# Pauses per quarter and layer in a Hyena and attention encoder layer, later transposes of k, and another order of casts where two Strassen runs begin

## The chip, the core and the metric

The kernel runs on one core of one Trainium2 chip, in one launch. The metric is the time of that launch on the device, in microseconds (us). The engines are TensorE (PE: matrix products and transposes), VectorE (DVE), ScalarE (ACT), GpSimd (POOL) and SyncE (SP, which issues the loads of weights). Each engine has its own queue and works through it in order; one waits for another through semaphores.

## What is computed

One layer of an encoder on 512 tokens of 2048 channels, in float32. The normalised input goes through one projection to a Hyena branch (three blocks of 1024 channels), to attention (8 heads of q, 2 of k and v, 128 wide) and to two blocks of gates.

```python
h = rms_norm(x, mix_norm_g)
u_h, q, k, v, g = split(h @ w_in)
x0, x1, hv = split(centred_short_conv(u_h, hy_conv_w, hy_conv_b))
filt = implicit_filter(S, ...)            # a 3-layer sine MLP, then w4 and a decay
z = hv * x1
z = bidir_fft_conv(z, filt) + hy_bias * z
y_h = z * x0
y_a = attention(axial_rope(rms_norm(q)), axial_rope(rms_norm(k)), v)
g_h, g_a = split(sigmoid(g + b_gate))
x = x + (g_h * (y_h @ w_br_hyena) + g_a * (y_a @ w_br_attn)) @ w_out
h2 = rms_norm(x, ffn_norm_g)
return x + (silu(h2 @ w_ffn_gate) * (h2 @ w_ffn_up)) @ w_ffn_down
```

## The kernel before

Every float32 operand is split into a high part (a cast on ScalarE) and a low part (the difference, on VectorE), and a product is three matmuls: high by high, high by low, low by high (`mm3`). Weights come from one packed tensor, in blocks of 128 x 1024, on SyncE's queue; a block's raw tile is `wr`, its parts are `wh` and `wl`. The matmuls stand on TensorE in the order in which the code issues them. The other engines' orders are made by a scheduler from the program's order, from priorities and from `behind(ins)`, which keeps an instruction behind another one.

The stages are, in order of time: the projection's first tiles `px` with the norm's sum beside them; the rest of the Hyena projection, `px`, tile by tile, and the last `phv`; the chunk `kv`; q's chunk for group 0, a pair of gates, q's chunk for group 1; the branches' products `b`; the rest of the gates, as a Strassen-Winograd scheme of seven products (`seven`, tiles `gx`, `gy`, `gz`); the output projection `o`; the FFN's gate and up projections in the same scheme (`fx`, `fy`, `fz`); and the FFN's down projection `d`, `e`.

Beside these main groups runs side work: generators in a queue, of which `step()` (L143) advances one after each `mm3` of a main group. `yield n` in a generator makes it wait until n steps have passed; a step is one triple of matmuls. Up to the kv chunk the side work is: `mlp_gen` (L307), the MLP of three layers that makes the filter, where `hp` is a layer's product, `ha` its argument and `h` its sine, with a pause `MLP_WAIT` ahead of each layer and behind the last; `taps_gen`, the products `fp` of the MLP's output with w4, and the decay (`fd`, `bd`); a pause; and then, for each of four quarters of the channels, `filter_gen` (transposes `ktp`, tiles `kt`, their splits `k..h` and `k..l`, then the spectra `kp`), and the convolution (`ztp`, `up`, the products `cu` and `cv` with the spectrum, their transposed splits `Yt`, then `ab`). The next quarter's taps lie inside the one before. The norm's factor is broadcast by four small matmuls `rs1bcp`, which ScalarE copies to `rbc`.

Behind the kv chunk the side queue is flushed, and the code issues in this order: VectorE's squares of the norm's factor; the split of v (`vh` on ScalarE, `vl` on VectorE, L770 to L776); `rope_tables` for k (L646: two loads on ScalarE's queue, `rpk` with 512 KB and `gaink` with 128 KB, then eight products on GpSimd); and `norm_rope` for k (L657: squares `kscr`, the root `krt`, `kqn`, and the rotation to `ko`, half of it on GpSimd). `rpk` takes memory that the convolution's pool leaves, so whichever of `vh` and `rpk` is first on ScalarE waits for the last of the quarters. `k_gen` (L700) is side work inside the q chunk: K_WAIT steps, then the transposes `kT0p` and `kT1p` of ko. `attend_gen` (L706) transposes q's heads and makes the scores `sp`, whose softmax is `p` on ScalarE; it is side work too.

In `run` (L950), the first group of a Strassen run is issued while its operands are still being made. `V` holds the seven sums of the activations of one pair of channel blocks, `X` their parts; the last pair is number 7. `x_high` and `x_low` split parts a to b of a pair; `wsum` adds two weight tiles (`gs`, `fs`), `wsplit` splits a tile (`gwhs`, `gwls`, `fwhs`, `fwls`), and `fold` copies one half of a bank on ScalarE and adds the other on VectorE (`gv`, `fv`). The run of the gates splits the last pair in two pieces, 0 to 3 and 3 to 7, at once; the run of the FFN gets its last pair only when `o` is done (`sums()`), and inside it the second norm is summed (`norm`, `token_rstd`: `rs2ss`, `rs2a`, a root on ScalarE with a table load, `rs2dg`).

Of the kernel before, what the change touches and what calls it, by code (L numbers as in the profile page):

```python
# [23 lines left out]
NQ = 4  # L24
# [8 lines left out]
HYENA_LAST = 0, 13, 14, 15  # L33
ATT_LAST = 4, 5, 6, 7, 0, 1, 2, 3
G_EARLY = 7
MLP_WAIT = 18
Z_WAIT0 = 16
N_WARM = 10
XW = 4
RS_STEP = 8  # L40
K_WAIT = 20
Q_WAIT = (27, 28)
S_WAIT0 = 6
S_WAIT = 2
# [70 lines left out]
def layer_kernel(tc, wpk, xT, par, flt, zemb, w4, decT, tb2, rope, qkg, out):  # L115
# [46 lines left out]
    def queue(gen):  # L162
        side["queue"].append(gen)

    def pause(n):
        yield n
# [140 lines left out]
    def mlp_gen():  # L307


        hcur = zem  # L310
        yield MLP_WAIT
        w4_load(0)
        for l in range(3):
            nk = 33 if l == 0 else 64
            nr = 64 if l < 2 else P
            hp = ps_tile(f"hp{l}")
            mm(hp[:nr], fl[:nk, l * 64:l * 64 + nr], hcur[:nk], True, True)
            a = tmp(f"ha{l}")[:nr]
            nn = tmp(f"hn{l}")[:nr]
            nc.vector.tensor_scalar(a, hp[:nr], fl[:nr, 256 + l:257 + l], fl[:nr, 259:260], ALU.add, ALU.mult)  # L320
            nc.vector.tensor_scalar(nn, a, float(np.float32(1 / (2 * math.pi))), MAGIC, ALU.mult, ALU.add)
            nc.vector.tensor_scalar(nn, nn, MAGIC, None, ALU.subtract)
            for c in (C1, C2, C3):
                nc.vector.scalar_tensor_tensor(a, nn, -c, a, ALU.mult, ALU.add)
            nc.vector.tensor_scalar(a, a, PI32, -PI32, ALU.min, ALU.max)
            hcur = tmp(f"h{l}")[:nr]
            nc.scalar.activation(hcur, a, AF.Sin)
            if l == 2:

                hh, hl = cw("hh", [P, S], "hh", dt=F32R), cw("hl", [P, S], "hl", dt=F32R)  # L330
                nc.scalar.copy(hh, hcur)
                nc.vector.tensor_tensor(hl, hcur, hh.bitcast(F32), ALU.subtract)
                mlp["h"] = hh, hl
            yield MLP_WAIT
            if l == 0:
                w4_parts(0)

# [57 lines left out]
    def filter_gen(q):  # L395
# [17 lines left out]
            yield 3  # L413
        if q + 1 < NQ:
            w4_parts(q + 1)
        yield 9

        kd[q] = dpool.tile([256, 6 * 256], F32, tag=f"kd{q}", bufs=1, name=f"kd{q}")
        spectra = [], []
# [31 lines left out]
    def conv_gen(q):  # L451
# [37 lines left out]
                yield 5  # L489
        if q + 1 < NQ:  # L490
            yield from taps_gen(q + 1)
        yield 11 if q + 1 < NQ else 14
        abs_ = [work(f"abs{2 * q + c}") for c in range(2)]
        for ph in range(2):
            ab = [ps_tile(f"ab{q}{ph}{c}") for c in range(2)]
# [32 lines left out]
    xg, acc1 = [], work("acc1")  # L528
    queue(mlp_gen())
    queue(taps_gen(0))  # L530
    queue(pause(18))
    queue(filter_gen(0))
    w00 = wblk()
    for k in range(KT):
# [171 lines left out]
    def attend_gen(g, qr):  # L706
# [3 lines left out]
        qT = []  # L710
        for h in range(4):
            qT.append(head_T(qr, h, "qTh", "qTl", 4, f"qT{g}{h}"))
            yield 2
        pr, pt = {}, {}

        def scores(u):
# [102 lines left out]
    def seven(nm, gi, nv=3, turns=False, early=NEARLY):  # L819
# [73 lines left out]
        def wsplit(w, name, ins=None, low_ins=None):  # L893
            hi = wpool.tile([P, BLK * P], F32R, tag="whi", bufs=3, name=f"{nm}wh{name}")
            lo = wpool.tile([P, BLK * P], F32R, tag="wlo", bufs=3, name=f"{nm}wl{name}")
            with behind(ins):
                nc.scalar.copy(hi, w)  # L897
            with behind(low_ins):
                raws["wl"] = nc.vector.tensor_tensor(lo, w, hi.bitcast(F32), ALU.subtract).ins  # L899
            return hi, lo  # L900
# [49 lines left out]
        def run(groups, c_tiles, finish, rows=None, sums=None, side_pool=None, norm=None, tail=None, each=None, halves=False,  # L950
# [17 lines left out]
            for n in range(groups):  # L968
# [8 lines left out]
                if first:  # L977
# [5 lines left out]
                    ready = NP - 1 if sums else NP  # L983
                    s1 = wsum(f"s1_{n}", w0["a21"], w0["a22"])
                    for p in range(early, ready):
                        x_split(p, V[p], (0, 7) if p < NP - 1 else (0, 3, 7))
                        if p == (early if sums else NP - 1):
                            s2 = wsum(f"s2_{n}", s1, w0["a11"], raws["xl"])
                    rest(raws["xl"] if sums else raws["sum"])
# [14 lines left out]
                elif not sums:  # L1004
                    s4 = wsum(f"s4_{n}", s2, w0["a12"], v1a)
                hs1 = wsplit(s1, f"s1_{n}", raws["x"] if first else None)
                if ready < NP:
                    product(y, hs1, 2, True, 0, ready, part="high")
                else:
                    product(y, hs1, 2, True, 0, ready, swap=turn(n))  # L1010
                if ready < NP:
                    V[ready] = sums()
                    v6 = raws["v6"]
                    x_split(ready, V[ready], (0, 3))
                    s4 = wsum(f"s4_{n}", s2, w0["a12"], v6)
                    x3 = raws["x"]
                    x_high(ready, V[ready], 3, 7)
                    product(x, h11, 0, True, ready)
                    product(y, hs1, 2, True, 0, ready, part="low")
                    product(y, hs1, 2, True, ready)  # L1020
                    v1 = fold(f"v1_{n}", x)
                    x_low(ready, V[ready], 3, 4, raws["folda"])
                    hs2 = wsplit(s2, f"s2_{n}", x3, raws["xl"])
                if first:
                    if early == NEARLY:
# [11 lines left out]
                if first and norm:  # L1037
                    with behind(raws["fold"]), behind(raws["folda"]):
                        acc_ins = norm()
                    x_low(NP - 1, V[NP - 1], 4, 7, acc_ins)  # L1040
                    rs2 = token_rstd(acc2, "rs2", {"bc": rbc2})
                    next(rs2)
                c0, c1 = c_tiles(n, late["cp"])
# [5 lines left out]
                product(y, hs4, 5, False, swap=turn(n))  # L1049
                read(v16, v16, y[:, :H], ALU.subtract)  # L1050
                read(c0[:, H:], v16, y[:, H:], ALU.subtract)
                s3 = wsum(f"s3_{n}", w0["a11"], w0["a21"], raws["folda" if norm else "v5a"] if first else None)
                product(x, wsplit(s3, f"s3_{n}"), 4, False, swap=turn(n))
                read(v5, v5, x[:, :H], ALU.subtract)
                read(c1[:, H:], v5, x[:, H:], ALU.subtract)
# [431 lines left out]
```

## Time and profile before

| | us |
|---|---|
| median of 3 runs | 2507.4 |
| lowest and highest | 2506.33, 2507.5 |
| the profiled execution | 2507.22 |
| its span, first to last instruction | 2505.4 |
| TensorE busy | 2491.3 (99%) |
| VectorE busy | 2087.1 (83%) |
| ScalarE busy | 1190.2 (48%) |
| GpSimd busy | 183.2 (7%) |

The clock that TensorE was granted is 1.000 over the whole span. A row of the timeline has the start in us from the span's start, the length, the engine, the line of the kernel, the operation, and the tiles as written <- read, with buffer numbers left out; `x4` is a run of four such instructions, and brackets name the idle time of the engine ahead of it and what ended it. "ACTq" is a load issued by ScalarE. A row of the waits has the instruction that waited, what it waited for, the total, the number of times and the longest.

### The profile page before, as it was taken

To read this page: it belongs to the slowest core of one execution; us is meant where nothing else is said; L and a number is where in the kernel's file an instruction comes from. 1 tells how busy PE (TensorE), PEld (TensorE's weight loads), DVE (VectorE), ACT (ScalarE), POOL (GpSimd) and SP (SyncE) were. 2 spreads that over 40 slices of the span, in tenths; PEclk is the share of its full clock that TensorE was granted. 3 is DMA by queue.
4 is the path that set the end of the run, shared out by engine and by line. 5 is a ranking of instruction groups with operands and counts; after the bars stand their busy time and mean duration, and the time that the engine had idled before them with its cause. 6 is when DMAs were issued, how large, how long until landed. Compare 5 with 4: busy or idle time off the path is not lost.

```text
span 2505.4 us, 34427 instructions
## 1 busy us (share of the span) xinstructions
PE 2491.3 (99%) x13114; PEld 2139.9 (85%) x13114; DVE 2087.1 (83%) x2968; ACT 1190.2 (48%) x1777; POOL 183.2 (7%) x295
## 2 busy tenths in 40 slices
PE   9999999999999999999999999999999999999999
PEld 7887888888888888888888888888888888888888
DVE  7898985755579999564999999999989988997988
ACT  6443334554455544443544444444444445445443
POOL 0000113020000000000000000000000002001111
PEclk9999999999999999999999999999999999999999
DMA  6434443223544444554333333333343448557754
GB/s 207 132 123 128 139 143 114 68 97 118 185 168 157 146 154 141 193 168 143 112 116 120 133 110 129 116 127 126 110 134 110 134 135 216 150 148 188 192 154 110
DMA packets 113538, 350.42 MB, mean 140 GB/s; under 512 B 13987, under 2 KB 15267, under 8 KB 113148
## 3 DMA queue, kind: packets, MB, share of 16 engines
q1 hardware_dynamic: 70128, 248.02, 30.1%
q0 software_dynamic: 22832, 63.19, 9.6%
q10 hardware_dynamic: 20412, 37.00, 4.8%
q8 instruction: 103, 1.69, 0.3%
q14 instruction: 63, 0.52, 0.1%
HBM read 297.56 MB, written 54.26 MB: 140 GB/s over the span
## 4 chain that ended last, share of the span: by engine, by line
PE 80%; DVE 1%; ACT 0%; issue 0%; ACTq 0%
PE fx L133 19%; PE fy L133 10%; PE b L133 7%; PE o L133 7%; PE gx L133 6%; PE d L133 5%; PE fz L133 5%; PE dx L133 4%; PE ex L133 3%; PE gy L133 3%; PE dy L133 2%; PE ey L133 2%; PE gz L133 2%; PE q L133 1%; PE dz L133 1%; PE av L133 1%
## 5 line engine op out<-in xcount | busy, mean ns | idle before, releaser
L189 DVE TENSOR_TENSOR wl<-wr,wh 128x1024 fp32r<-128x1024 f32 (+1 forms) x168 | 200.8, 1195 | 112.6 <-ACT wh L188 112.3
L188 ACT CAST wh<-wr 128x1024 fp32r<-128x1024 f32 (+1 forms) x168 | 173.1, 1031 | 227.4 <-PE o L133 67.1
L897 ACT CAST fwhs<-fs 128x1024 fp32r<-128x1024 f32 x176 | 184.6, 1049 | 89.1 <-PE fz L133 73.8
L899 DVE TENSOR_TENSOR fwls<-fs,fwhs 128x1024 fp32r<-128x1024 f32 x176 | 214.3, 1218 | 4.3 <-ACT fwhs L897 4.2
L897 ACT CAST fwha<-fa 128x1024 fp32r<-128x1024 f32 x132 | 138.9, 1053 | 149.8 <-PE fx L133 83.2
L133 PE MATMUL px<-xh,wh 128*128 128x512 f32 x576 | 180.1, 394 | 1.5 <-ACT rbc L270 0.7
L133 PE MATMUL fx<-fX,fwhs 128*128 128x512 f32 x704 | 175.3, 391 | 1.2 <-ACT fwhs L897 1.0
L133 PE MATMUL fy<-fX,fwhs 128*128 128x512 f32 x704 | 175.4, 391 | 0.0
L133 PE MATMUL fx<-fX,fwha 128*128 128x512 f32 x704 | 171.9, 391 | 0.0
L899 DVE TENSOR_TENSOR fwla<-fa,fwha 128x1024 fp32r<-128x1024 f32 x132 | 161.2, 1221 | 10.0 <-ACT fwha L897 9.7
L133 PE MATMUL o<-ms,wh 128*128 128x512 f32 x512 | 157.7, 389 | 0.0
L133 PEld LDWEIGHTS fx<-fX,fwhs 128*128 128x128 f32 x704 | 129.2, 188 | 26.7 <-ACT fwhs L897 1.2
L133 PEld LDWEIGHTS fx<-fX,fwha 128*128 128x128 f32 x704 | 129.3, 188 | 25.0
L133 PEld LDWEIGHTS fy<-fX,fwhs 128*128 128x128 f32 x704 | 129.3, 188 | 24.9
L133 PEld LDWEIGHTS px<-xh,wh 128*128 128x128 f32 x576 | 106.4, 188 | 26.4 <-issue 2.4
L133 PE MATMUL d<-act,wh 128*128 128x512 f32 x384 | 118.2, 389 | 0.0
L133 PEld LDWEIGHTS o<-ms,wh 128*128 128x128 f32 x512 | 96.1, 188 | 19.8
L133 PE MATMUL px<-xh,wl 128*128 128x512 f32 x288 | 112.6, 391 | 0.0
L890 DVE TENSOR_TENSOR fs<-fa,fa 128x1024 f32<-128x1024 f32 x88 | 107.1, 1217 | 1.7 <-PE o L133 1.0
L890 DVE TENSOR_TENSOR fs<-fs,fa 128x1024 f32<-128x1024 f32 x88 | 107.3, 1219 | 0.9 <-PE o L133 0.2
L133 PE MATMUL o<-ms,wl 128*128 128x512 f32 x256 | 99.6, 389 | 0.0
L133 PE MATMUL fx<-fX,fwls 128*128 128x256 f32 x704 | 98.6, 283 | 0.2 <-DVE fwls L899 0.2
(970 smaller groups left out, 5897.6 us busy)
## 6 DMA issues: line engine op xcount, KB each, us to landing
fa<-wpk SPq DMA_DIRECT2D x176, 512.0 KB, 3.9
wr<-wpk SPq DMA_DIRECT2D x162, 512.0 KB, 3.5
ga<-wpk SPq DMA_DIRECT2D x60, 512.0 KB, 4.4
da<-wpk SPq DMA_DIRECT2D x32, 512.0 KB, 3.9
ea<-wpk SPq DMA_DIRECT2D x32, 512.0 KB, 4.2
actd<-c POOLq DMA_DIRECT2D x41, 256.0 KB, 4.3
actr<-actd ACTq DMA_DIRECT2D x41, 256.0 KB, 4.1
x2d<-dt POOLq DMA_DIRECT2D x32, 256.0 KB, 5.8
```

Of the source, the lines that this page charges most:

```text
L133: tc.keep_in_program_order(nc.tensor.matmul(out, lhsT=lhsT, rhs=rhs, start=start, stop=stop, **kw))
L188: nc.scalar.copy(st["hi"][:, c], st["raw"][:, c])
L189: nc.vector.tensor_tensor(st["lo"][:, c], st["raw"][:, c], st["hi"][:, c].bitcast(F32), ALU.subtract)
L890: raws["sum"] = nc.vector.tensor_tensor(t, a, b, ALU.add).ins
L897: nc.scalar.copy(hi, w)
L899: raws["wl"] = nc.vector.tensor_tensor(lo, w, hi.bitcast(F32), ALU.subtract).ins
```

## The change

Five kinds of edits. The MLP's pauses become 14, 20, 20 and 26 steps in place of four times 18, and the pause behind the first taps 16 in place of 18. The pause between a quarter's transposes `ktp` and its spectra becomes 8, 8, 11, 8 in place of 9, and the one ahead of `ab` 11, 13, 11, 14 in place of 11, 11, 11, 14. K_WAIT becomes 23 in place of 20, and in group 0 two steps more lie ahead of the first scores. In the gates' first group the last pair's parts 3 to 7 are cast behind the high part of the first weight sum, not ahead of it. In the FFN's first group only part 3 of the last pair is cast ahead of the first fold, and parts 4 to 7 behind it; and the third weight sum is added right behind the last pair's low parts, ahead of the norm's chain, in place of behind the fourth product's fold.

```diff
...
-MLP_WAIT = 18
+MLP_WAITS = 14, 20, 20, 26
...
-K_WAIT = 20
+TURN_WAIT = 8, 8, 11, 8
+Y_WAIT = 11, 13, 11, 14
+K_WAIT = 23
...
 
 
         hcur = zem
-        yield MLP_WAIT
+        yield MLP_WAITS[0]
         w4_load(0)
         for l in range(3):
             nk = 33 if l == 0 else 64
...
                 nc.scalar.copy(hh, hcur)
                 nc.vector.tensor_tensor(hl, hcur, hh.bitcast(F32), ALU.subtract)
                 mlp["h"] = hh, hl
-            yield MLP_WAIT
+            yield MLP_WAITS[l + 1]
             if l == 0:
                 w4_parts(0)
 
...
             yield 3
         if q + 1 < NQ:
             w4_parts(q + 1)
-        yield 9
+        yield TURN_WAIT[q]
 
         kd[q] = dpool.tile([256, 6 * 256], F32, tag=f"kd{q}", bufs=1, name=f"kd{q}")
         spectra = [], []
...
                 yield 5
         if q + 1 < NQ:
             yield from taps_gen(q + 1)
-        yield 11 if q + 1 < NQ else 14
+        yield Y_WAIT[q]
         abs_ = [work(f"abs{2 * q + c}") for c in range(2)]
         for ph in range(2):
             ab = [ps_tile(f"ab{q}{ph}{c}") for c in range(2)]
...
     xg, acc1 = [], work("acc1")
     queue(mlp_gen())
     queue(taps_gen(0))
-    queue(pause(18))
+    queue(pause(16))
     queue(filter_gen(0))
     w00 = wblk()
     for k in range(KT):
...
         qT = []
         for h in range(4):
             qT.append(head_T(qr, h, "qTh", "qTl", 4, f"qT{g}{h}"))
-            yield 2
+            yield 2 if g or h < 3 else 4
         pr, pt = {}, {}
 
         def scores(u):
...
             hi = wpool.tile([P, BLK * P], F32R, tag="whi", bufs=3, name=f"{nm}wh{name}")
             lo = wpool.tile([P, BLK * P], F32R, tag="wlo", bufs=3, name=f"{nm}wl{name}")
             with behind(ins):
-                nc.scalar.copy(hi, w)
+                raws["wh"] = nc.scalar.copy(hi, w).ins
             with behind(low_ins):
                 raws["wl"] = nc.vector.tensor_tensor(lo, w, hi.bitcast(F32), ALU.subtract).ins
             return hi, lo
...
                     ready = NP - 1 if sums else NP
                     s1 = wsum(f"s1_{n}", w0["a21"], w0["a22"])
                     for p in range(early, ready):
-                        x_split(p, V[p], (0, 7) if p < NP - 1 else (0, 3, 7))
+                        x_split(p, V[p], (0, 7) if p < NP - 1 else (0, 3))
                         if p == (early if sums else NP - 1):
                             s2 = wsum(f"s2_{n}", s1, w0["a11"], raws["xl"])
                     rest(raws["xl"] if sums else raws["sum"])
...
                 elif not sums:
                     s4 = wsum(f"s4_{n}", s2, w0["a12"], v1a)
                 hs1 = wsplit(s1, f"s1_{n}", raws["x"] if first else None)
+                if first and ready == NP:
+                    with behind(raws["wh"]):
+                        x_high(NP - 1, V[NP - 1], 3, 7)
+                    x_low(NP - 1, V[NP - 1], 3, 7, raws["wl"])
                 if ready < NP:
                     product(y, hs1, 2, True, 0, ready, part="high")
                 else:
...
                     x_split(ready, V[ready], (0, 3))
                     s4 = wsum(f"s4_{n}", s2, w0["a12"], v6)
                     x3 = raws["x"]
-                    x_high(ready, V[ready], 3, 7)
+                    x_high(ready, V[ready], 3, 4)
                     product(x, h11, 0, True, ready)
                     product(y, hs1, 2, True, 0, ready, part="low")
                     product(y, hs1, 2, True, ready)
                     v1 = fold(f"v1_{n}", x)
                     x_low(ready, V[ready], 3, 4, raws["folda"])
+                    with behind(raws["fold"]):
+                        x_high(ready, V[ready], 4, 7)
                     hs2 = wsplit(s2, f"s2_{n}", x3, raws["xl"])
                 if first:
                     if early == NEARLY:
...
                     with behind(raws["fold"]), behind(raws["folda"]):
                         acc_ins = norm()
                     x_low(NP - 1, V[NP - 1], 4, 7, acc_ins)
+                    s3 = wsum(f"s3_{n}", w0["a11"], w0["a21"], raws["xl"])
                     rs2 = token_rstd(acc2, "rs2", {"bc": rbc2})
                     next(rs2)
                 c0, c1 = c_tiles(n, late["cp"])
...
                 product(y, hs4, 5, False, swap=turn(n))
                 read(v16, v16, y[:, :H], ALU.subtract)
                 read(c0[:, H:], v16, y[:, H:], ALU.subtract)
-                s3 = wsum(f"s3_{n}", w0["a11"], w0["a21"], raws["folda" if norm else "v5a"] if first else None)
+                if not (first and norm):
+                    s3 = wsum(f"s3_{n}", w0["a11"], w0["a21"], raws["v5a"] if first else None)
                 product(x, wsplit(s3, f"s3_{n}"), 4, False, swap=turn(n))
                 read(v5, v5, x[:, :H], ALU.subtract)
                 read(c1[:, H:], v5, x[:, H:], ALU.subtract)
```

With the pauses the instructions move against each other. On TensorE, at the end of the first `px` group behind the projection's start, the broadcast of the norm stood behind four products of taps (`fp`, eight matmuls, of which the last two are seen); the rows before:

```order
L133 MATMUL px_560<-xh_507,wh_614 128x512 x2
L133 MATMUL px_560<-xh_507,wl_615 128x512
L133 MATMUL px_560<-xh_533,wh_614 128x512 x2
L133 MATMUL px_560<-xh_533,wl_615 128x512
L133 MATMUL fp_679<-hh,w4s_367 128x512
L133 MATMUL fp_679<-hl,w4s_367 128x512
L133 MATMUL rs1bcp<-rs1dg,rs1ones 128x128 x4
L133 MATMUL px_729<-xh_130,wh_731 128x512 x2
```

And now:

```order
L135 MATMUL px_560<-xh_507,wh_614 128x512 x2
L135 MATMUL px_560<-xh_507,wl_615 128x512
L135 MATMUL px_560<-xh_533,wh_614 128x512 x2
L135 MATMUL px_560<-xh_533,wl_615 128x512
L135 MATMUL rs1bcp<-rs1dg,rs1ones 128x128 x4
L135 MATMUL px_689<-xh_130,wh_691 128x512 x2
L135 MATMUL px_689<-xh_130,wl_692 128x512
L135 MATMUL px_689<-xh_151,wh_691 128x512 x2
```

The first four products of taps now stand behind the broadcast `rs1bcp`, inside the next `px` group, which also has another bank.

On ScalarE, behind the last casts of the convolution (`abl` and a weight block), the rows with the table of k (`rpk`, `gaink`), the splits of v (`vh`) and the squares of k (`kscr`), before:

```order
L510 ACTIVATE abl_3460<-ab_3428,rn_2746 128x256
L188 CAST wh_3660<-wr_3659 128x1024
L650 DMA rpk<-rope 128x1024
L651 DMA gaink<-qkg 128x256
L774 ACTIVATE vh_3514<-kv_3096,rs1ry 128x256
L774 ACTIVATE vh_3518<-kv_3097,rs1ry 128x256
L665 ACTIVATE kscr_3543,kss<-kv_3096 128x128 x2
L774 ACTIVATE vh_3522<-kv_3098,rs1ry 128x256
L665 ACTIVATE kscr_3547,kss<-kv_3097 128x128
L188 CAST wh_3690<-wr_3689 128x1024
L774 ACTIVATE vh_3526<-kv_3099,rs1ry 128x256
```

And now:

```order
L190 CAST wh_3660<-wr_3659 128x1024
L512 ACTIVATE abl_3484<-ab_3454,rn_2730 128x256
L512 ACTIVATE abl_3487<-ab_3455,rn_2776 128x256
L776 ACTIVATE vh_3514<-kv_3053,rs1ry 128x256
L776 ACTIVATE vh_3518<-kv_3054,rs1ry 128x256
L190 CAST wh_3690<-wr_3689 128x1024
L776 ACTIVATE vh_3522<-kv_3055,rs1ry 128x256
L776 ACTIVATE vh_3526<-kv_3056,rs1ry 128x256
L652 DMA rpk<-rope 128x1024
L653 DMA gaink<-qkg 128x256
L667 ACTIVATE kscr_3543,kss<-kv_3053 128x128 x2
L667 ACTIVATE kscr_3547,kss<-kv_3054 128x128 x2
```

The two loads have moved from ahead of the four `vh` to behind them, and a weight block's cast (`wh_3690`) stands ahead of them too.

On VectorE, in the FFN's first group, from the last pair's low parts (`fX`, 128x3x256) on; `fs` are sums of weights, `fwls` their low parts, `fv` a fold and `rs2a` the norm's first step. Before:

```order
L279 TENSOR_TENSOR acc_9886<-acc_9886,x2sq_10944 128x512
L860 TENSOR_TENSOR fX_10893<-fV_10883,fX_10893 128x3x256
L258 TENSOR_SCALAR rs2a<-rs2ss 128x4
L899 TENSOR_TENSOR fwls_0_10976<-fs_0_10896,fwhs_0_10975 128x1024
L943 TENSOR_TENSOR fv_0_10972<-fx_10857,fv_0_10972 128x256
L890 TENSOR_TENSOR fs_0_10997<-fa_0_10808,fa_0_10810 128x1024
L948 TENSOR_TENSOR fv_0_10972<-fv_0_10972,fy_10856 128x256
L225 RECIPROCAL rs2ry<-rs2rt 128x4
```

And now:

```order
L281 TENSOR_TENSOR acc_9886<-acc_9886,x2sq_10945 128x512
L862 TENSOR_TENSOR fX_10893<-fV_10883,fX_10893 128x3x256
L892 TENSOR_TENSOR fs_0_10949<-fa_0_10808,fa_0_10810 128x1024
L945 TENSOR_TENSOR fv_0_10975<-fx_10857,fv_0_10975 128x256
L260 TENSOR_SCALAR rs2a<-rs2ss 128x4
L901 TENSOR_TENSOR fwls_0_10979<-fs_0_10896,fwhs_0_10978 128x1024
L901 TENSOR_TENSOR fwls_0_11001<-fs_0_10949,fwhs_0_11000 128x1024
L227 RECIPROCAL rs2ry<-rs2rt 128x4
```

The sum of `fa_0_10808` and `fa_0_10810` has moved from behind `fwls_0_10976` and the fold to right behind the low parts, and the fold and the sum now stand ahead of that `fwls` (`fwls_0_10979` now).

## Prediction

> **What bounds the kernel now.** I read the page's busy shares first, then the waits of TensorE, then its timeline at the stalls.
>
> ```profile
> PE 2491.3 (99%) x13114; PEld 2139.9 (85%) x13114; DVE 2087.1 (83%) x2968; ACT 1190.2 (48%) x1777; POOL 183.2 (7%) x295
> ```
>
> TensorE (PE) is busy for 2491.3 us of a span of 2505.4. The change adds and removes no matmul, so all it can win is PE's idle time, 14.1 us, a part of which is the start and the tail. The waits of PE say whom it waited for (total, times, longest):
>
> ```profile
> PE kp L133 <- ACT k021h L209: 1.2, 1, 1.2
> PE warm L133 <- DVE wones L246: 1.1, 1, 1.1
> PE fx L133 <- ACT fwhs L897: 1.0, 1, 1.0
> PE kT0p L136 <- DVE ko L688: 1.0, 2, 0.6
> PE ab L133 <- DVE cu L482: 0.9, 1, 0.9
> PE px L133 <- ACT rbc L270: 0.7, 1, 0.7
> PE hp L133 <- ACT h L327: 0.6, 1, 0.6
> PE gy L133 <- ACT gwhs L897: 0.6, 1, 0.6
> PE px L133 <- DVE fd L370: 0.5, 1, 0.5
> PE sp L133 <- ACT p L728: 0.5, 2, 0.3
> PE ab L133 <- DVE Yt311l L210: 0.3, 1, 0.3
> PE fx L133 <- DVE fwls L899: 0.2, 1, 0.2
> PE up L133 <- DVE zt21l L210: 0.2, 1, 0.2
> PE px L133 <- ACT xh L539: 0.2, 1, 0.2
> PE kp L133 <- DVE k021l L210: 0.2, 1, 0.2
> PE fx L133 <- DVE fv L943: 0.2, 1, 0.2
> PE gx L133 <- DVE gv L943: 0.2, 1, 0.2
> ```
>
> Nearly every row is a place that the change touches. Without the warm-up these are 8.5 us in 18 waits, but a stall costs more than its row. PE's timeline shows why (start, length, idle before in brackets):
>
> ```profile
> 247.69 0.50 PE L133 MATMUL kp<-k021h,CS 128*128 128x512 f32 x1 [1.23 <-ACT k021h L209]
> 248.41 0.50 PE L133 MATMUL kp<-k021l,CS 128*128 128x512 f32 x1 [0.23 <-DVE k021l L210]
> 248.75 0.39 PE L133 MATMUL kp<-k021h,CS 128*128 128x512 f32 x1
> 248.98 0.63 PE L133 MATMUL px<-xh,wh 128*128 128x512 f32 x2
> ```
>
> Unhindered, the next 512-column matmul starts 0.23 us after the one before (248.75 to 248.98), though each lasts 0.39, since they overlap. The second kp here started 0.72 after the first and its successor 0.34 after it: 0.49 + 0.11 = 0.60 us lost where the view says 0.23. From this and from shorter stalls I price a stall at its row + 0.27 us (0.2 to 0.4). All 18 together then cost 8.5 + 4.9 = 13.4 us: the most that can be won. A step of the side work, one triple of matmuls, is 3 x 0.227 = 0.68 us.
>
> **The change, part by part.** The sum is made against the profiled run's 2507.2 us, 0.2 below the median of the runs.
>
> The filter MLP's pauses. hp0 starts 4 steps (2.72 us) sooner, hp1 2 steps (1.36): hp1's operand comes 1.36 us sooner relative to it, more than the 0.6 us wait. Gain 0.6 + 0.27 = 0.9. If ScalarE's casts of x push the sine back, it is 0.3.
>
> The norm's broadcast. The MLP now ends 8 steps later and the pause behind it is 2 shorter, so the first four tap products (fp, eight matmuls) move behind rs1bcp, and px's next group takes another PSUM bank: it no longer waits for rbc, only for a weight that has long been cast. Gain 0.7 + 0.27 = 1.0. VectorE then does the taps' work later, against the first filter's transposes: I take off 0.15 (0 to 0.6).
>
> The conv quarters. Counted in steps, the side work sits +5 (q0), +4, then +6 (q1), +8 (q2) and +7 (q3) against the main groups. The 0.9 wait (ab of q1 for cu) and the 1.4 (kp of q2, two waits) get two steps, 1.36 us, of their own each: gains 0.9 + 0.27 and about 1.75. Three small waits (px for fd 0.5, ab for Yt311l 0.3, up for zt21l 0.2: 1.8 with their stalls) get no pause of their own; the shift may clear or move them, and q0, q1 and q3 lose a step between transposes and kp. I take 0.6 of these. Gain 3.5; bounds 1.0 (the waits move on to the next place) and 4.9.
>
> k's transposes. K_WAIT puts them 3 steps (2.05 us) later, and two stalls stand there:
>
> ```profile
> 393.66 0.38 PE L136 MATMUL kT0p<-ident,ko 128*128 128x128 f32 x2
> 394.63 0.33 PE L136 MATMUL kT0p<-ident,ko 128*128 128x128 f32 x1 [0.59 <-DVE ko L688]
> 395.36 0.33 PE L136 MATMUL kT0p<-ident,ko 128*128 128x128 f32 x1 [0.40 <-DVE ko L688]
> ```
>
> At 0.11 us each the fourth would start at 394.0; it starts at 395.36, so 1.4 us is lost. Three steps would cover that, if ko came when it comes now. But the conv quarters end 7 steps later, and with that the order on ScalarE turns over: the loads of k's rotary table (rpk, gaink) stood ahead of the casts of v and now stand behind all four vh, with the cast of a weight block among them that waits for the last kv matmul.
>
> ```profile
> 375.42 0.33 ACTq L650 DMA_DIRECT2D rpk<-rope  x1
> ...
> 379.70 1.07 ACT L188 CAST wh<-wr 128x1024 fp32r<-128x1024 f32 x1
> 380.64 0.51 ACT L774 ACTIVATE vh<-kv,rs1ry 128x256 fp32r<-128x256 f32 x1
> ```
>
> A load does not overtake a waiting instruction ahead of it on its engine: this w4r left only when yh had waited 4.90 us.
>
> ```profile
> 239.35 0.82 ACT L575 ACTIVATE yh<-x04u,prm 128x512 f32<-128x512 f32 x1 [4.90 <-DVE x04u L574]
> 239.44 0.47 ACTq L344 DMA_DIRECT2D w4r<-w  x1
> ```
>
> So rpk leaves between 379.7 (the cast's start) and 381.7 (all vh done, two of about 0.45 behind a cast that ends at 380.77), say 380.2, against 375.42. How long the table takes, and what follows it, stands in these rows: GpSimd's eight products on it (least, median and longest ns, first and last start), then the same for q's table, its issue and GpSimd's start:
>
> ```profile
> L654 POOL TENSOR_TENSOR rpk<-rpk,gaink x8: 449/454/1403, 380.9 to 384.8; 128x128 f32<-128x128 f32 x8
> ```
>
> ```profile
> 394.85 0.33 ACTq L650 DMA_DIRECT2D rpq<-rope  x1
> ```
>
> ```profile
> 398.35 2.71 POOL L654 TENSOR_TENSOR rpq<-rpq,gainq 128x128 f32<-128x128 f32 x4 [4.26 <-DVE kT0l L210]
> ```
>
> From issue to GpSimd's start it was 5.5 us for k (375.42 to 380.9) and 3.5 for q; I take the middle, 4.5. The eight products took 4.3, to 385.3. Behind them stood the last squares of k, the root krt, and in the end the last ko:
>
> ```profile
> 385.70 0.28 ACT L665 ACTIVATE kscr<-kv 128x128 f32<-128x128 f32 x1 [3.77 <-POOL rpk L654]
> ```
>
> ```profile
> 386.62 0.21 ACT L224 ACTIVATE krt<-kss 128x8 f32<-128x8 f32 x1 [0.29 <-DVE kss L666]
> ```
>
> ```profile
> 394.88 0.42 DVE L688 TENSOR_TENSOR ko<-ko,kt 128x256 f32<-128x256 f32 x1
> ```
>
> From 385.3 to the last ko's end (395.3) it was 10.0; the squares, 385.7 to 386.6, will be done by then, which leaves 9.1. So the last ko comes at 380.2 + 4.5 + 4.3 + 9.1 = 398.1, and PE wants it at 394.0 + 2.05 = 396.05: a stall of 2.05 + 0.27, 2.3, in place of 1.4. Loss 0.9 (a gain of 0.6 with 379.7 and 3.5; a loss of 3.4 with 381.7 and 5.5). The Trainium skill (DMA: Bandwidth & Descriptors, section "Anatomy of one DMA — SWDGE (gpsimd) path") puts a transfer at about 2.0 us + bytes / 436e3; for the 512 KB table that is an estimate of 3.2 us, and by it this term would be a gain of 0.4 and the forecast 2498.2. The trace has 5.5 and 3.5 for the same size, on another queue and with weights in flight, so I stay with its rows.
>
> The first scores. Two more steps (1.36 us) against two waits of 0.5 in all: both go. Gain 0.5 + 2 x 0.27 = 1.0.
>
> The gates' start. The last pair's high parts are cast around gwhs, not ahead of it, so gy's first weight comes about 1 us sooner: 0.6 + 0.27 and 0.2 + 0.27 = 1.3 go. But VectorE's second half of that pair then stands ahead of gv and of the next gwls: I expect two new waits of 0.1 to 0.2 us, 0.5 at the price of stalls. Gain 0.8 (0 to 1.3).
>
> The FFN's start. The third sum (fs, 1.2 us on VectorE) now comes before the norm instead of behind fwls, so its cast no longer stands behind the table load: the fx waits (1.0, 0.2) and, since three quarters of a cast are taken from ahead of the first copy, the 0.2 for fv go: 1.4 + 3 x 0.27 = 2.2. What is late next is the fwls that the sum now precedes:
>
> ```profile
> 1205.51 0.16 DVE L258 TENSOR_SCALAR rs2a<-rs2ss 128x4 f32<-128x4 f32 x1 [0.68 <-PE rs2ss L133]
> 1205.59 1.22 DVE L899 TENSOR_TENSOR fwls<-fs,fwhs 128x1024 fp32r<-128x1024 f32 x1
> ```
>
> ```profile
> 1207.27 1.11 PE L133 MATMUL fy<-fX,fwls 128*128 128x256 f32 x8
> ```
>
> It was ready at 1206.8, half a microsecond before PE read it. The sum takes as long as that fwls, 1.2, and fills the 0.68 of idle time, so fwls comes 0.5 later, at 1207.3 (the fold that also goes ahead and the earlier start of the row about cancel), while PE, rid of the first stall, wants it at 1206.8: 0.3 to 0.5 + 0.27, some 0.6. Gain 1.6 (0.8 to 2.2).
>
> The sum: 0.9 + 1.0 - 0.15 + 3.5 - 0.9 + 1.0 + 0.8 + 1.6 = 7.75 us, and 2507.2 - 7.75 = 2499.5.
>
> **The rivals.** First, k's table is in time: it lands so that kT0p's stall goes. Then 1.4 + 0.9 = 2.3 us more are won: 2497.2. For it speaks q's 3.5; against it, that even 3.5 after the earliest issue leaves a few tenths, and that k's table took 5.5 with weights loading beside it. Second, the stalls only move: VectorE is 83% busy, and the pauses of the quarters hand a backlog to the next place. Then the quarters give 1.0, the two Strassen starts half of theirs (0.4 and 0.8), and the sum is 0.9 + 0.85 + 1.0 - 0.9 + 1.0 + 0.4 + 0.8 = 4.05: 2503.2. Against it speaks that the two largest waits get two steps each and that nothing else is asked of VectorE. Third, on the other side: k's table comes so late that it eats all. rpk leaves at 381.7, takes 5.5, and the eight products all run at 1403 ns, as the longest of them did, not at the median 454: 11.2 us. The last ko is then at 381.7 + 5.5 + 11.2 + 9.1 = 407.5, the stall 11.45 + 0.27, 10.3 more than now, against 8.65 won elsewhere: 2508.9; and 2512.6 if the stalls also only move and 4.95 are won. It decides from a stall of 10 us at kT0p, a last ko later than 405.8. The Trainium skill (GPSIMD Engine Reference, "1. Specifications") says that GpSimd's SBUF interfaces are shared with VectorE and contend with its instructions of two SBUF inputs; the row would agree if that was the one product of 1403. Against this rival: the median of the eight is 454, and VectorE has little to do while k's chain waits.
>
> **How the numbers follow.** Chances: forecast 0.55 (2497.6 to 2502.2 by the bounds of its terms, which will not all fall on one side), table in time 0.17, stalls move 0.24, other side 0.04. The likeliest is 2499.5. The range reaches past the first two rivals, each with half a microsecond or more for its own terms: 2496.6 to 2505.2; that leaves out the other side and the ends of the rest. About 0.2% (5.0 us, so 2502.4 and 2512.4) is what a measurement of this kernel can tell from no change. Faster by more than that: 0.9 of the forecast, all of the first rival, a tenth of the second, 0.69; slower: half of the third, 0.02; the rest, 0.29, within it.
>
> **What would show it.** In the changed kernel's waits of PE the rows for k021h, cu, rbc, h, p and the 1.0 for fwhs should be gone; kT0p for ko should have grown, to about 1.8 us in the view, with rpk's issue behind the first vh casts on ScalarE; and a small wait of fy for fwls should be new. Wrong would be: kT0p's row gone or above 4 us, waits of 1 us at other lines of the conv quarters, or matmuls that take longer than now.

## The result and the profile after

The changed kernel takes 2501.0 us (median of 15 runs, 2499.97 to 2503.99) against 2507.4 (15 runs): a ratio of 0.9977, 95% interval 0.9969 to 0.9985. That is 6.4 us less, where 7.9 less was predicted (2499.5), and inside the predicted range. Ten of the 15 runs lie at 2501.5 or below and five at 2502.9 or above, and nothing here shows what makes these two levels. The profiled execution took 2500.47 us, 6.75 less than the one of before.

TensorE's busy time in the changed kernel:

```profile
PE 2489.6 (100%) x13114; PEld 2141.0 (86%) x13114; DVE 2086.6 (84%) x2968; ACT 1191.1 (48%) x1778; POOL 181.0 (7%) x295
```

It has the same matmuls, and its span is 6.7 us shorter, so what went is idle time (14.1 us before, 9.1 now) and what stalls add to the matmuls beside them. The waits of TensorE, all of them:

```profile
PE warm L135 <- DVE wones L248: 1.1, 1, 1.1
PE kT0p L138 <- DVE ko L690: 1.0, 1, 1.0
PE kp L135 <- DVE k031l L212: 0.8, 1, 0.8
PE ktp L138 <- DVE hs L391: 0.7, 1, 0.7
PE gx L135 <- ACT gv L944: 0.5, 1, 0.5
PE sp L135 <- ACT p L730: 0.4, 1, 0.4
PE gx L135 <- DVE gwls L901: 0.2, 1, 0.2
PE fy L135 <- DVE fwls L901: 0.2, 1, 0.2
```

The 17 rows of before have become 8. Gone are the rows for k021h, cu, rbc, h, fwhs, gwhs, fd and Yt311l. Five rows are new. Those of gx for gwls and fy for fwls had been forecast; three had not, and no edit was meant for them: kp of the last quarter (k031l), the first transposes ktp, and a gx in the gates' second group that the view puts down to gv (e7 shows what it waits for). kT0p's wait is there still, with one stall in place of two. By the price of the prediction (row + 0.27 us) the seven waits without the warm-up cost 3.8 + 1.9 = 5.7 us, 7.7 less than the 13.4 of before; the two executions differ by 6.75. Over so many waits the price is good to an us.

At k's transposes, the changed kernel's timeline shows the chain: VectorE's last yh of the quarters; on ScalarE the first vh and the load of the table behind it; GpSimd's products; and on TensorE the first matmul of the q chunk and the transposes.

```profile
374.51 0.69 DVE L526 TENSOR_TENSOR yh<-yh,y 128x512 f32<-128x512 f32 x1
```

```profile
375.36 0.47 ACT L776 ACTIVATE vh<-kv,rs1ry 128x256 fp32r<-128x256 f32 x1 [3.56 <-DVE yh L526]
375.56 0.33 ACTq L652 DMA_DIRECT2D rpk<-rope  x1
```

```profile
379.43 4.38 POOL L656 TENSOR_TENSOR rpk<-rpk,gaink 128x128 f32<-128x128 f32 x8 [25.14 <-DVE kss L668]
```

```profile
375.30 0.39 PE L135 MATMUL q<-wh,xh 128*128 128x512 f32 x1
...
391.63 0.49 PE L138 MATMUL kT0p<-ident,ko 128*128 128x128 f32 x3
393.10 0.33 PE L138 MATMUL kT0p<-ident,ko 128*128 128x128 f32 x1 [0.99 <-DVE ko L690]
```

The table left 0.26 us behind the q chunk's first matmul; before, it left 3.96 us ahead of it (375.42 and 379.38). The second to fourth vh had not run yet: the load was issued once the first had ended its wait. GpSimd started 3.9 us behind rpk's issue: rpk had landed after 3.2 us, and gaink, issued 0.36 us later, after 3.3. The last transpose came 1.1 us late (393.10, and 391.96 unhindered).

### The profile page after: what moved, and what is told of

It reads as the page before. It is cut to its first block, busy times and chain, and to the rows that moved or that the text cites. A ratio compares the mean times of both kernels' runs of the same rounds, so it can differ in the third digit from the quotient of the medians.

```text
span 2498.7 us, 34436 instructions
## 1 busy us (share of the span) xinstructions
PE 2489.6 (100%) x13114; PEld 2141.0 (86%) x13114; DVE 2086.6 (84%) x2968; ACT 1191.1 (48%) x1778; POOL 181.0 (7%) x295
## 4 chain that ended last, share of the span: by engine, by line
PE 94%; DVE 4%; issue 1%; ACT 1%; DMA 1%; POOL 0%; ACTq 0%; POOLq 0%; DVEq 0%; SPq 0%
PE fx L135 19%; PE fy L135 10%; PE b L135 7%; PE o L135 7%; PE px L135 7%; PE gx L135 7%; PE d L135 5%; PE fz L135 5%; PE dx L135 4%; PE ex L135 3%; PE gy L135 3%; PE q L135 3%; PE phv L135 3%; PE dy L135 2%; PE ey L135 2%; PE gz L135 2%
## 5 line engine op out<-in xcount | busy, mean ns | idle before, releaser
L135 PE MATMUL fy<-fX,fwls 128*128 128x256 f32 x704 | 98.7, 283 | 0.2 <-DVE fwls L901 0.2
```

Source lines behind the costliest of these rows:

```text
L135: tc.keep_in_program_order(nc.tensor.matmul(out, lhsT=lhsT, rhs=rhs, start=start, stop=stop, **kw))
```

## The experiments

The runs of the kernel before beside them were 2507.4 to 2507.6 us in the median.

**e1: k's table first.** From the changed kernel:

```diff
+    rpk = rope_tables(1, "k")
     vs = []
...
-    queue(k_gen(norm_rope(kvp, 2, rope_tables(1, "k"), "k")))
+    queue(k_gen(norm_rope(kvp, 2, rpk, "k")))
```

> The changed kernel, with k's rotary table (both loads and GpSimd's products) issued ahead of the split of v, so that its loads stand ahead of all four vh on ScalarE again. Theory as predicted (the loads are late because they stand behind the vh): the stall at kT0p, 1.0 us in the view, goes, and the time falls by 1.1 to 1.3 us against the changed kernel, to about 2499.8. Rival, from the trace after (rpk left 0.2 us behind the start of the first vh, at 375.56, as soon as VectorE's last yh of the quarters was done, at 375.2): the loads wait for the end of the quarters, whichever comes first, so they leave some 0.3 us sooner, the stall shrinks by 0.3 and the time stays within 0.4 us of the changed kernel's 2501.0.

Measured: 2500.6 us (2499.5 to 2500.9), ratio 0.9973 (0.9962 to 0.9983). kT0p's wait is no shorter:

```profile
PE kT0p L138 <- DVE ko L690: 1.3, 1, 1.3
```

The last yh and the load, and on TensorE the start of the q chunk:

```profile
375.16 0.69 DVE L526 TENSOR_TENSOR yh<-yh,y 128x512 f32<-128x512 f32 x1
```

```profile
375.93 0.33 ACTq L652 DMA_DIRECT2D rpk<-rope  x1
```

```profile
375.40 0.39 PE L135 MATMUL q<-wh,xh 128*128 128x512 f32 x1
```

With the loads ahead of all vh, rpk leaves 0.08 us after yh's end, where the changed kernel has 0.36 (375.20 to 375.56), and still 0.5 behind the q chunk's start. The theory of the prediction falls: the order of the loads and the vh is worth 0.3 us at the load, and nothing that the time shows. What moved the table is the end of the quarters, whose memory it takes. The kernel before and e2 and e4, where the loads also stand first, have the same 0.08 to 0.09 us behind their last yh.

**e2: the attention's pauses alone**, on the kernel before:

```diff
-K_WAIT = 20
+K_WAIT = 23
...
-            yield 2
+            yield 2 if g or h < 3 else 4
```

> The kernel before with only K_WAIT 23 and the two steps more ahead of the first scores. Theory: with the quarters ending where they did, k's table comes as before, so three steps (2.05 us) cover the 1.4 us at kT0p, and the waits of sp shrink as they did in the changed kernel (0.4 to 1.0 us won): 2505.0 to 2505.7, and no row of kT0p in the waits of TensorE. Rival (the stalls only move): another wait of an us appears behind it and the time stays at 2506.5 or more.

Measured: 2505.7 us (2504.1 to 2507.3), ratio 0.9994 (0.9985 to 1.0003): 1.7 less, as expected, though within what the interval can't tell from none. In the profile kT0p has no row, and sp keeps one:

```profile
PE sp L133 <- ACT p L728: 0.4, 1, 0.4
```

Where the quarters end early, three steps clear k's stall.

**e3: the pauses of the MLP and the quarters alone**, on the kernel before (MLP_WAITS, TURN_WAIT, Y_WAIT and the pause of 16 as in the change):

```diff
-MLP_WAIT = 18
+MLP_WAITS = 14, 20, 20, 26
+TURN_WAIT = 8, 8, 11, 8
+Y_WAIT = 11, 13, 11, 14
```

> The kernel before with only the pauses of the MLP, the taps and the quarters changed; K_WAIT stays at 20. Theory: the gains of the MLP (0.9), of the norm less the new wait of ktp (0.0) and of the quarters (4.2) come, but the quarters now end 7 steps later, so the stall at kT0p, with 2.05 us less room than in the changed kernel, is 2.8 to 3.2 us in the view: 5.1 - 1.9 = 3.2 won, about 2504.2. Rival (k's chain is bound by something that goes with the q chunk, not by the end of the quarters): kT0p keeps its 1.0 us and the time is about 2502.3.

Measured: 2506.7 us (2504.0 to 2510.6), ratio 0.9997 (0.9988 to 1.0006). Up to the q chunk the pauses win 3.9 us: its first matmul starts at 375.52, and at 379.38 before. Behind it 4.1 us are given back, 2.5 of them at kT0p, where the last transpose comes 3.8 us late in place of 1.4:

```profile
PE kT0p L138 <- DVE ko L690: 3.2, 3, 1.7
```

```profile
376.48 0.33 ACTq L652 DMA_DIRECT2D rpk<-rope  x1
```

```profile
375.52 0.39 PE L135 MATMUL q<-wh,xh 128*128 128x512 f32 x1
```

The table leaves 0.96 us behind the q chunk's start. The rival with its unchanged 1.0 us is out. The time is some 2 us above the theory's, and the profile shows 1.6 of them: right behind kT0p's last wait the clock that TensorE is granted falls to half for some 3 us. The mean over the stretch from 395 to 396 us is the third number from the end, 0.50, and two matmuls of 512 columns take 0.85 us from start to start (395.03 to 395.88), where they take 0.45 at the full clock:

```profile
395.03 1.05 PE L135 MATMUL q<-wh,xh 128*128 128x512 f32 x2
395.88 0.63 PE L135 MATMUL q<-wl,xh 128*128 128x512 f32 x1
```

```profile
395.00:396.00 1.00, 1.00 (x4) 0.77 (x3) 0.69 (x1) 0.00 (x0) 0.00 (x0) 0.50 0.88 348
```

Seven of the 11 runs of e3 have a mean clock of 0.998 or 0.999 and took 2506.6 to 2510.6 us; the four at 1.000 took 2504.0 to 2505.6, close to the theory. That the three waits, 3.2 us within some 4, bring the clock down is likely and not shown; single waits of up to 1.7 us (e11) did not.

**e4: the two Strassen starts alone** (the changed kernel with all pauses as before):

```diff
-MLP_WAITS = 14, 20, 20, 26
+MLP_WAITS = 18, 18, 18, 18
-TURN_WAIT = 8, 8, 11, 8
-Y_WAIT = 11, 13, 11, 14
-K_WAIT = 23
+TURN_WAIT = 9, 9, 9, 9
+Y_WAIT = 11, 11, 11, 14
+K_WAIT = 20
```

> The kernel before with only the two Strassen starts changed (order of casts in the gates' first group and the FFN's, third sum ahead of the norm). Theory: the FFN's start wins 1.9, the gates' 0.7, and the new wait of gx for gv in the gates' second group (0.5 in the view, 0.6 as a stall) comes with the edit itself, since the scheduler then puts two casts of weights ahead of that fold: 2.0 won, about 2505.4. Rival (that wait belongs to the later start of something else, not to the edit): it is absent here, and 2.6 are won: 2504.8.

Measured: 2505.4 us (2504.4 to 2507.8), ratio 0.9994 (0.9985 to 1.0003): 2.0 less, as the theory had it, though the interval can't tell it from none, and the new wait is there:

```profile
PE gx L135 <- ACT gv L944: 0.4, 1, 0.4
```

Here the quarters end as in the kernel before, and the table leaves 3.94 us ahead of the q chunk (375.48 and 379.42), like there.

**e5: K_WAIT 28**, on the changed kernel:

```diff
-K_WAIT = 23
+K_WAIT = 28
```

> The changed kernel with K_WAIT 28 in place of 23: k's transposes stand 5 steps (3.4 us) later in the q chunk, nothing else moves. Theory (the last ko comes 18 us after the first matmul of the q chunk, because the quarters end just ahead of it): kT0p leaves the waits of TensorE and 1.2 us are won against the changed kernel, about 2499.8. Rival (some instruction that follows on the transposes is then late): a new wait in the q chunk or at the first scores, and no gain, 2501.

Measured: 2499.0 us (2498.5 to 2501.2), ratio 0.9966 (0.9954 to 0.9979). kT0p is gone, and nothing has come behind it:

```profile
PE warm L135 <- DVE wones L248: 1.1, 1, 1.1
PE kp L135 <- DVE k031l L212: 0.8, 1, 0.8
PE kp L135 <- ACT k031h L211: 0.4, 1, 0.4
PE sp L135 <- ACT p L730: 0.4, 1, 0.4
PE gx L135 <- DVE gwls L901: 0.4, 1, 0.4
PE ktp L138 <- DVE hs L391: 0.3, 1, 0.3
```

From the first matmul of the q chunk to that of the branches' products it takes 141.3 us, where the changed kernel takes 142.5: the 1.2 of the theory. It is the fastest median of the study. Its interval overlaps the changed kernel's, but four of its five runs lie below every run of that kernel.

**e6: the MLP's pauses back**, the quarters where the change puts them:

```diff
-MLP_WAITS = 14, 20, 20, 26
+MLP_WAITS = 18, 18, 18, 18
...
-    queue(pause(16))
+    queue(pause(24))
```

> The changed kernel with the MLP's pauses back at 18 each, and the pause behind the taps lengthened from 16 to 24 so that the quarters stay where they are. Theory (the MLP's pauses won 0.9 at hp and 1.0 at the norm's broadcast, and cost 0.9 at the first transposes ktp, which come too close behind the taps): the waits of hp and of px for rbc are back, ktp's is gone, and the time rises by 0.9 us to about 2501.9. Rival (ktp's wait comes from the work of the quarters on VectorE, not from the taps' place): ktp stays and the time rises by 1.8, to 2502.8.

Measured: 2500.7 us (2500.3 to 2501.4), ratio 0.9971 (0.9960 to 0.9982). Neither theory: ktp is gone and rbc is back, but the time didn't rise, since hp did not come back.

```profile
PE px L135 <- ACT rbc L272: 0.7, 1, 0.7
```

The profiles of e2 and e4, with the MLP's pauses of before, have no row for hp either. Its 0.6 us stood in the one profile that the prediction was read from. ktp's wait varies as well: 0.3 to 0.7 us in the other profiles with the MLP's pauses of the change, and no row in e8, e9 and e10.

**e7: the gates' order of casts back**, on the changed kernel:

```diff
-                        x_split(p, V[p], (0, 7) if p < NP - 1 else (0, 3))
+                        x_split(p, V[p], (0, 7) if p < NP - 1 else (0, 3, 7))
...
-                if first and ready == NP:
-                    with behind(raws["wh"]):
-                        x_high(NP - 1, V[NP - 1], 3, 7)
-                    x_low(NP - 1, V[NP - 1], 3, 7, raws["wl"])
```

> The changed kernel with the order of casts in the gates' first group as before. Theory (the edit wins 0.75 in the first group and loses 0.6 in the second, where the scheduler now puts two casts of weights ahead of the fold of gy): the two waits of gx change into those of before (gy for gwhs, gx for gv), the wait in the second group goes, and the time stays within 0.3 us of the changed kernel. Rival (the second group's wait is from elsewhere): it stays, and the time rises by 0.7, to 2501.7.

Measured: 2501.0 us (2500.5 to 2506.5), ratio 0.9976 (0.9967 to 0.9985): the changed kernel's time. The waits of the gates are those of before, and the one in the second group is gone, as the theory had it, but not for its reason. The theory took that wait for one on the fold of gy, since the view names gv. In e11, the same kernel, the fold's copy ends 0.06 us behind the start of this matmul (749.41 and 749.35), so the matmul can't have waited for it, and the view names gwls:

```profile
749.04 0.37 ACT L944 COPY gv<-gy 128x256 f32<-128x256 f32 x1
```

```profile
749.35 1.19 PE L135 MATMUL gx<-gX,gwls 128*128 128x256 f32 x8 [0.39 <-DVE gwls L901]
```

In both profiles the matmul starts 0.14 us behind the end of gwls, the low part of the second weight sum. In the changed kernel VectorE makes it behind the third sum, although its cast ended at 744.88:

```profile
745.85 1.22 DVE L892 TENSOR_TENSOR gs<-ga,ga 128x1024 f32<-128x1024 f32 x1
...
747.92 1.22 DVE L901 TENSOR_TENSOR gwls<-gs,gwhs 128x1024 fp32r<-128x1024 f32 x1
```

```profile
749.28 1.18 PE L135 MATMUL gx<-gX,gwls 128*128 128x256 f32 x8 [0.46 <-ACT gv L944]
```

In e7 VectorE makes it ahead of the third sum (753.37), and it is ready 2.6 us before TensorE reads it:

```profile
748.53 1.22 DVE L901 TENSOR_TENSOR gwls<-gs,gwhs 128x1024 fp32r<-128x1024 f32 x1
```

```profile
752.34 1.12 PE L135 MATMUL gx<-gX,gwls 128*128 128x256 f32 x8
```

The profiled execution of e7 was its slowest, 2506.5 us, and shows waits at places that the edit doesn't touch, and behind that of ab the clock at 0.50 once more, from 300 to 303 us:

```profile
PE ex L135 <- DVE ev L945: 1.5, 1, 1.5
...
PE ab L135 <- DVE cu L484: 1.0, 1, 1.0
...
PE ey L135 <- DVE ev L945: 0.7, 1, 0.7
```

**e8: more room, partly taken elsewhere**, on the changed kernel:

```diff
-TURN_WAIT = 8, 8, 11, 8
-Y_WAIT = 11, 13, 11, 14
-K_WAIT = 23
+TURN_WAIT = 8, 8, 11, 10
+Y_WAIT = 11, 13, 11, 12
+K_WAIT = 28
...
-    queue(pause(16))
+    queue(pause(18))
...
-            yield 2 if g or h < 3 else 4
+            yield 2 if g or h < 3 else 5
```

> The changed kernel with more room at each wait that is left: K_WAIT 28, the pause behind the taps 18 (from 16), the last quarter's pauses 10 and 12 in place of 8 and 14, and one step more ahead of the first scores. Theory (each of these waits is a lack of steps at its place): kT0p (1.2), kp for k031l (1.0), ktp (0.9) and sp (0.5) shrink or go, 3.0 to 3.6 won, 2497.4 to 2498.0. Rival (VectorE's backlog hands them on): new waits in the quarters, and 1.2 or less is won beside kT0p, 2499 or more.

Measured: 2500.7 us (2499.5 to 2502.7), ratio 0.9971 (0.9960 to 0.9982). The rival: kT0p, ktp and sp are gone, kp is down to 0.2, and the two steps taken from ab of the last quarter cost all of it:

```profile
PE ab L135 <- ACT Yt310h L211: 1.2, 1, 1.2
PE warm L135 <- DVE wones L248: 1.1, 1, 1.1
PE ab L135 <- DVE Yt311l L212: 0.7, 1, 0.7
PE ab L135 <- DVE Yt310l L212: 0.7, 1, 0.7
```

**e9: the same room, none taken**: as e8, but Y_WAIT as in the change and K_WAIT 34.

```diff
-TURN_WAIT = 8, 8, 11, 8
+TURN_WAIT = 8, 8, 11, 10
-K_WAIT = 23
+K_WAIT = 34
...
-    queue(pause(16))
+    queue(pause(18))
...
-            yield 2 if g or h < 3 else 4
+            yield 2 if g or h < 3 else 5
```

> The changed kernel with steps added, and none taken: K_WAIT 34, the pause behind the taps 18 (from 16), the last quarter's pause ahead of kp 10 (from 8) with 14 kept ahead of ab, and one step more ahead of the first scores. Theory (what kept e8 from its gain was the last quarter's pause ahead of ab, cut from 14 to 12: four waits of 3.7 us as stalls): ktp, kT0p and sp leave the waits, kp shrinks to 0.3, no wait of ab for Yt31 of more than 0.5 in all, and 3 us are won against the changed kernel run beside it: 2497.5 to 2498.3. Rival (the quarters are now so late that their end stands bare behind the kv chunk): a wait of 1 us or more between the last ab and the q chunk, and no more than e5 won, 2499.

Measured: 2499.5 us (2498.4 to 2500.9), ratio 0.9970 (0.9958 to 0.9981), 1.1 below the changed kernel beside it (e11): no more than K_WAIT alone. The theory's 3 us did not come, and neither did the wait that the rival named, between the last ab and the q chunk. The wait of ab is smaller, and another has come:

```profile
PE ab L135 <- DVE Yt311l L212: 0.7, 1, 0.7
...
PE px L135 <- DVE fd L372: 0.5, 1, 0.5
```

With the steps added, VectorE's work of the quarters is late elsewhere: for the quarters the second rival of the prediction (the stalls only move) seems to hold from here on.

**e10: the third sum back**, on the changed kernel:

```diff
-                    s3 = wsum(f"s3_{n}", w0["a11"], w0["a21"], raws["xl"])
...
-                if not (first and norm):
-                    s3 = wsum(f"s3_{n}", w0["a11"], w0["a21"], raws["v5a"] if first else None)
+                s3 = wsum(f"s3_{n}", w0["a11"], w0["a21"], raws["folda" if norm else "v5a"] if first else None)
```

> The changed kernel with the third weight sum of the FFN's first group back behind the fold, the order of the last pair's casts as changed. Theory (the place of the sum is what won at the FFN's start: the fx wait of 1.0 for fwhs and the 0.2 for fwls stood there because the sum came last): both are back, 1.6 us as stalls, the 0.2 of fy for fwls (0.3 as a stall) goes, and the time rises by 1.3 us against the changed kernel run beside it. Rival (the earlier fold, from the last pair's cast in two pieces, won it): the time rises by 0.3 or less.

Measured: 2502.1 us (2501.0 to 2503.0), ratio 0.9980 (0.9971 to 0.9989), 1.5 above the changed kernel beside it; the intervals overlap, but from the first matmul of the output projection to the end it takes 1483.5 us, and 1482.1 in both profiles of the changed kernel. Both waits are back, and that of fy, 0.2 in the first profile, has no row (nor has it in e11):

```profile
PE fx L135 <- ACT fwhs L899: 1.0, 1, 1.0
...
PE fx L135 <- DVE fwls L901: 0.2, 1, 0.2
```

The place of the sum is what wins at the FFN's start.

**e11: the changed kernel again**, on the chip of e9 and e10, unedited.

> The changed kernel itself, on the chip of the two others, as their yardstick and for what varies from run to run. Theory (hp's wait in the one profile of before, the wait of ab for cu and the two levels of the changed kernel's times come with single executions): about 2501.0, with waits of its profile that differ from those of the first profile only at tiles that wait for loads (ab for cu) by up to 1 us. Rival (the differences between the experiments' profiles are the edits' own): the same waits as in the first profile.

Measured: 2500.6 us (2500.3 to 2503.1), ratio 0.9975 (0.9966 to 0.9985). Its profile has the same waits but for fy's, two of them with other sizes, and none at cu:

```profile
PE kT0p L138 <- DVE ko L690: 1.7, 1, 1.7
```

kT0p's wait, 1.0 there, is 1.7 here, and ktp's 0.4 against 0.7; the gates' two waits are both put down to gwls here. Neither statement holds as written: waits vary from one execution to the next, and not only at ab for cu. kT0p's follows the table: rpk leaves 0.26 us behind the q chunk's start in the first profile and 1.10 here (0.53 and 0.59 in e1 and e6, where the wait is 1.3), and from rpk's issue to the last ko's end it is 17.4 to 17.6 us in the changed kernel, e1, e3, e5, e6, e7, e10 and e11 alike.

## Why the prediction was right

The sum held to 1.5 us, and there is luck in that. From the first matmul of a stage to that of the next, the two profiles of the changed kernel win this against the profile of before:

| stage | terms | predicted | won | won, e11 |
|---|---|---|---|---|
| start to q's chunk | MLP, norm, quarters | 5.25 | 4.1 | 5.0 |
| q's chunk to the branches | k's transposes, first scores | 0.1 | 0.75 | 0.0 |
| branches to output projection | gates | 0.8 | 0.1 | -0.1 |
| output projection to the end | FFN | 1.6 | 1.8 | 1.8 |

The stages add up to 6.7 in both. The quarters' share of the first row can be told apart: the q chunk starts at 379.38, 377.70 and 379.42 in the profiles of before, e2 and e4, 378.8 in the mean, and at 374.37 to 375.52, 375.0 in the mean, in those of the changed kernel, e1, e3, e5, e10 and e11. e6, with the MLP's pauses of before, has 375.35. So the quarters won about 3.8, the norm and the MLP about nothing, as far as executions up to 1.7 us apart can tell.

The two large terms, the quarters and the FFN's start, came by the mechanism that was given for them: at the FFN e10 shows it; in the quarters the rows for k021h and cu went where steps were added, and the q chunk starts that much sooner, but no experiment takes the single stalls of the quarters apart. At the FFN the fwls that the sum now precedes is the new wait that was named, 0.15 us for the 0.3 to 0.5 predicted:

```profile
1202.20 1.21 PE L135 MATMUL fy<-fX,fwls 128*128 128x256 f32 x8 [0.15 <-DVE fwls L901]
```

In the quarters the wait of kp for k031l stands where "q0, q1 and q3 lose a step between transposes and kp" had put a doubt; it was given no price of its own. In e8 and e9, with two steps more there, it shrinks from 0.8 to 0.2.

The step that failed in its reason is "with that the order on ScalarE turns over", at k's table. The order did turn over, but e1 shows that it costs 0.3 us at the load and no time that can be measured; the loads wait for the quarters' memory in either order, and e3 against the kernel before shows what decides: with the quarters' end 7 steps later the table leaves 0.96 us behind the q chunk's start in place of 3.96 ahead of it, and kT0p waits 3.2 us in place of 1.0. The sizes were not far off. Against the q chunk's start the last ko was put at 18.7 us and came at 17.75: the table left 0.6 sooner than assumed (+0.26, not +0.82) and took 3.9 us, not 4.5. A loss of 0.9 became a gain of 0.2 (the last transpose 1.1 us late in place of 1.4), or a loss of 0.5 in e11 (1.9 late). The formula of the Trainium skill (DMA: Bandwidth & Descriptors, "Anatomy of one DMA — SWDGE (gpsimd) path"), an estimate of 3.2 us, agrees with the 3.2 that the table took to land here, and not with the 4.8 of before. What it leaves out is the second load, for which GpSimd also waited.

Four smaller terms were mis-sized, and they promised some 3 us too much; that the last ko came sooner than forecast, and that the quarters and the FFN won a little more, made good a part of it. The MLP's came from one execution's profile. The norm's was offset by ktp, for which up to 0.6 had been allowed and 0.15 taken. Of the scores' waits one stayed. And for the gates the cost was sought in the first group only, while the scheduler also moved the sums in the second: the order of the instructions would have shown that row.

Of the rivals, the first (table in time) and the third (table far too late) are out. The second held in part: ktp and k031l are new stalls, 1.5 us in the view, but the two large terms kept their gains; e8 and e9 show where more steps stop helping. The third rested on one slow product of eight on GpSimd, 1403 ns. It ran beside VectorE's subtraction for a weight block (380.95, and 380.80 to 382.03), and so did the slow one of the changed kernel, 1439 ns (382.37, and 382.03 to 383.49); in e9, with no such subtraction beside them, all eight took 448 to 462 ns.

## What to carry to other kernels

When side work is given room by pauses, follow its end: what is allocated behind it (here a table in memory that it leaves) moves by the sum of all pauses, and a pause at that later place (e5, one number) wins back what the earlier ones cost there. Steps for one wait are safe where they are added, and not where they are taken from a neighbour (e8). Where several waits of about a microsecond stand close together, look at the granted clock behind them (e3). And a stall of half a microsecond that stands in one profile should be looked for in a second one before it is counted as a gain.

## What the runs showed of the hardware

A load on ScalarE's queue can be issued while compute instructions that stand ahead of it have not run: in the changed kernel rpk was issued at 375.56, ahead of three of the four vh, of which the second started at 375.73. No load was seen to pass an instruction that still waited: w4r, in the kernel before, left 0.09 us behind the start of one that had waited 4.90 us.

The clock that TensorE is granted fell from 1.00 to 0.50 for some 3 us in two profiles, each time right behind waits of TensorE that stood close together: e3 (0.8, 0.7 and 1.7 us at kT0p) and e7 (0.3 and 1.0 us at ab). Single waits of 1.7 us (kT0p in e11) and 1.5 us (ex in e7) passed without it. What decides stays open.

The same load of 512 KB, k's table, landed 4.8 us after its issue in the kernel before and 3.2 in the changed one; what makes the difference stays open.
